# Linear attention beside softmax attention: two projections beside each of the first attention blocks, then stages of the linear attention beside the other blocks

## The chip, the cores and the metric

The kernel runs on one core of one Trainium2 chip. The metric is the device time of one execution in microseconds (us). A core has a matrix engine (PE in the profile; its loads of stationary operands are the engine PEld), a vector engine (DVE), a scalar engine for functions and copies (ACT), a general engine (POOL), and a queue that issues DMAs (SP). Each engine works through its own list of instructions in order, and waits where an operand isn't there yet. SBUF is the working memory of 128 partitions, PSUM the memory that PE writes into.

## The reference

One step of a two-layer network over 128 context tokens and 1024 latent tokens (1152 columns in all), width 1024, float32. The change lies in layer 0, whose mixer is this:

```python
def even_lat(h, kc, vc, s0, w_in, sink, w_alpha, b_alpha, gla_gain, w_out):
    qa, ka, va, qb, kb, vb, rb, lr = even_project(h, w_in)          # one projection, split
    oa = latent_attention(rope_2d(qa), rope_2d(ka), va, kc, vc, sink)   # 8 heads, blocks of 128
    ob, _, _ = gla_bidir(qb, kb, vb, lr, w_alpha, b_alpha, s0[:, 0], s0[:, 1])   # 4 heads
    return jnp.concatenate([oa, gla_output(ob, rb, gla_gain)], axis=-1) @ w_out

def gla_chunked(q, k, v, log_a, s0):          # chunks of 64 tokens, once forward, once backward
    bcum = jnp.cumsum(ac, axis=3)
    q_e, k_e, k_s = qc * exp(bcum), kc * exp(-bcum), kc * exp(b_last - bcum)
    attn = where(mask, einsum('nbhid,nbhjd->nbhij', q_e, k_e), 0)
    o_intra = einsum('nbhij,nbhjv->nbhiv', attn, vc)
    kv = einsum('nbhjd,nbhjv->nbhdv', k_s, vc)
    # scan over the chunks: o_inter = q_e @ s;  s = decay_last * s + kv
    return o_intra + o_inter, s_fin

def gla_output(o, r, gain):                   # o: tokens x 4 heads x 128
    o = o * rsqrt(mean(o * o, axis=-1) + EPS)
    return o.reshape(B, T, B_WIDTH) * gain * silu(r)
```

Every layer also has shifts, scales and gates from a map of the conditioning vector (48 units of the matrix `w_ada`), and a feed-forward part after the mixer.

## The kernel before

Activations lie with the features on partitions and the 1152 tokens along the free side, as 128 x 1152 tiles in slots `u0` to `u33`. A projection (`proj`) is three chunks of 384 tokens, each 24 matmuls (lines 148 to 150: float32 is split into a high and a low part, three products per 128 features), into one of three PSUM buffers `mm`.

The stretch that the change touches comes after the first projections:

- A loop of nine calls, `attention(i - 1)` for the context block and the eight latent blocks. A call takes two groups of four heads through score matmuls (L777 to L789, into `S`), mask and maximum (L794), exponentials (L803), division (L810), transposes (L815, into `X`), a split into high and low part (`split`, L144 and L145) and the products with the values (L826 to L828, into the one buffer `O`). Beside each of the first eight calls stands one projection with `ev_spill` (the q and k of the linear attention, then its gates r), which goes to HBM, and two units of the conditioning map (`ada_step(2)`). The projections read `H`, which holds slots u0 to u15.
- The linear attention (GLA) of four heads, each in stages. `gla_a` loads q, k, v and the decays, forms the scaled keys (ACT, POOL), transposes them and makes the chunk states KV (L902, L917, copies L929 on ACT and DVE). `gla_b` scans the states over the chunks: four DVE scans of 64 x 1152 (L943, L944), two for each half of the value width. `gla_c` makes the products within the chunks (L963), masks them (L966), and sums them with the products of the states (L972, L975) in `O`. `gla_d` squares the result, sums over the 128 features by a matmul with ones, takes the root, spreads it over partitions by a matmul (`rstd_r` L230, `rstd_b` L240), and multiplies by gain and by silu of the gate. Before the change only `gla_a(0)` stands in the loop, in its last round; the rest follows it, with units of the conditioning map (`ada_step(6)`) and the output product of the softmax heads (`out_a`, four calls of 72 matmuls with residual adds, `resid`, L318) in between.
- A unit of the conditioning map (`ada_unit`) loads two 512 KB pieces of `w_ada` into a ring of buffers, five before the change (three of the tiles `raw`, which `wload` also uses for weights, and c0, c1), and does eight small matmuls (L193) and two with the matrix `sel` (L199). Forty units run in this stretch: eighteen in the loop, the others after it.

The program is written in that order, but a scheduler of the framework sets the order of the instructions on each engine, by its own timing model and by which buffers are free, and puts in all waits. The order it made is fixed in the program.

## Time and profile before

| | us |
|---|---|
| median of 3 runs (2879.07 to 2884.31) | 2879.49 |
| the profiled execution | 2881.95 |
| its span in the trace | 2880.2 |
| PE busy / DVE busy / ACT busy / POOL busy in the span | 2712.5 / 2023.1 / 1329.0 / 1277.9 |
| mean granted clock of TensorE, of full speed | 0.957 |

The profile page lists for each engine how long it was busy; a PE record lasts longer than the distance to the next one, since matmuls overlap, so the work of PE is read from the starts of successive instructions. Tables by stretch give the busy time of each engine, the number of its instructions, and PEclk, the granted clock of TensorE as a share of its full speed (1.00 is 2.4 GHz, 0.50 is 1.2 GHz).

### The profile page before, as it was taken

Reading aid. Unit: us, or ns where it says so; the run is one execution under the profiler, and the core shown is the slowest. Engines: PE = TensorE matmul, PEld = TensorE weight load, DVE = VectorE, ACT = ScalarE, POOL = GpSimd, SP = SyncE. Lnnn points to the kernel's source line nnn. Section 1 sums busy time; section 2 is a strip of 40 time slices with the busy share of each in tenths; the row PEclk is TensorE's granted clock in tenths of the full one; section 3 lists DMA queues with packets and bytes.
Section 4 is the critical chain, followed back from the end, with each engine's and each line's share of the span. In section 5 each row is a group of like instructions: output and inputs, shape, how many; then the busy total and the mean of one; then the engine's idle time right before and its main releaser. Section 6 shows DMA issues by size and latency. Waiting matters only on the chain.

```text
span 2880.2 us, 48645 instructions
## 1 busy us (share of the span) xinstructions
PE 2712.5 (94%) x18792; PEld 2608.1 (91%) x18792; DVE 2023.1 (70%) x3509; ACT 1329.0 (46%) x2329; POOL 1277.9 (44%) x768
## 2 busy tenths in 40 slices
PE   7999997989899999999999989786899999999998
PEld 5888885878899999999999989786899999999998
DVE  5465667554588778778777565657788877787876
ACT  5445555533544444435335566574543433444333
POOL 4230005222655555456555433333455556455453
PEclk9999997788999999999999999998999999999999
DMA  7124347444153222623223123364342233423322
GB/s 272 64 91 162 122 134 258 146 148 147 67 204 104 81 88 89 227 81 94 90 88 125 54 89 114 122 224 145 112 170 85 87 98 108 171 88 105 104 82 70
DMA packets 138120, 353.67 MB, mean 123 GB/s; under 512 B 14720, under 2 KB 64256, under 8 KB 137888
## 3 DMA queue, kind: packets, MB, share of 16 engines
q1 hardware_dynamic: 136160, 343.48, 36.2%
q0 software_dynamic: 1728, 7.08, 0.7%
q8 instruction: 148, 2.42, 0.3%
q14 instruction: 84, 0.69, 0.1%
HBM read 286.20 MB, written 64.30 MB: 122 GB/s over the span
## 4 chain that ended last, share of the span: by engine, by line
PE 73%; DVE 11%; ACT 6%; DMA 5%; issue 3%; POOL 1%; SPq 0%; DVEq 0%; ACTq 0%; POOLq 0%
PE mm L148 10%; PE mm L150 10%; PE mm L149 10%; PE X L148 5%; PE X L150 5%; PE X L149 5%; PE S L148 4%; PE S L150 4%; PE S L149 4%; PE O L148 2%; PE O L150 2%; PE O L149 2%; PE mm L193 1%; DMA raw<-in_w_fi_dram 1%; PE O L975 1%
## 5 line engine op out<-in xcount | busy, mean ns | idle before, releaser
L150 PE MATMUL mm<-u,w 128*128 128x384 f32 (+1 forms) x1320 | 424.3, 323 | 1.9 <-DVE w L459 1.9
L148 PE MATMUL mm<-u,w 128*128 128x288 f32 (+1 forms) x1234 | 401.4, 326 | 22.0 <-DVE u L318 21.7
L149 PE MATMUL mm<-u,w 128*128 128x288 f32 (+1 forms) x1234 | 396.8, 322 | 2.7 <-POOL u L145 2.7
L140 POOL TENSOR_TENSOR w<-raw,w 128x1024 fp32r<-128x1024 f32 (+1 forms) x66 | 148.8, 2254 | 369.7 <-ACT w L139 319.3
L148 PEld LDWEIGHTS mm<-u,w 128*128 128x128 f32 x1234 | 238.8, 194 | 28.9 <-issue 26.0
L150 PEld LDWEIGHTS mm<-u,w 128*128 128x128 f32 x1320 | 253.7, 192 | 6.0 <-issue 3.5
L149 PEld LDWEIGHTS mm<-u,w 128*128 128x128 f32 x1234 | 238.5, 193 | 3.4 <-POOL u L145 2.9
L150 PE MATMUL mm<-u,u 128*128 128x288 f32 x693 | 204.5, 297 | 0.0
L148 PE MATMUL S<-u,w 128*128 128x288 f32 (+1 forms) x526 | 163.6, 311 | 40.7 <-ACT t L1173 35.0
L318 DVE SCALAR_TENSOR_TENSOR u<-mm,mods,u 128x288 f32<-128x288 f32 (+4 forms) x345 | 146.6, 453 | 76.9 <-PE mm L150 76.4
L150 PE MATMUL X<-u,w 128*128 128x288 f32 (+1 forms) x630 | 192.0, 306 | 0.0
L148 PE MATMUL mm<-u,u 128*128 128x288 f32 x627 | 187.6, 299 | 3.7 <-ACT u L445 3.5
L149 PE MATMUL mm<-u,u 128*128 128x288 f32 x627 | 186.3, 297 | 0.0
L148 PE MATMUL X<-u,w 128*128 128x288 f32 (+1 forms) x580 | 175.9, 305 | 3.0 <-DVE u L145 2.4
L149 PE MATMUL X<-u,w 128*128 128x288 f32 (+1 forms) x580 | 175.5, 304 | 0.0
L149 PE MATMUL S<-u,w 128*128 128x288 f32 (+1 forms) x526 | 162.2, 308 | 0.0
L148 PE MATMUL mm<-u,c 128*128 128x288 f32 (+2 forms) x497 | 152.6, 307 | 0.7 <-DVE ta L506 0.7
L149 PE MATMUL mm<-u,c 128*128 128x288 f32 (+2 forms) x497 | 151.6, 305 | 0.4 <-POOL u L145 0.4
L452 POOL TENSOR_TENSOR u<-raw 128x512 f32<-128x512 f32 x82 | 133.4, 1627 | 34.4 <-DMA raw<-in_w_fi_dram 19.3
L148 PEld LDWEIGHTS S<-u,w 128*128 128x128 f32 x526 | 100.8, 192 | 43.5 <-ACT t L1173 37.1
L448 DVE TENSOR_TENSOR u<-u,raw 128x512 f32<-128x512 f32 x82 | 138.2, 1685 | 0.8
L148 PE MATMUL X<-u,u 128*128 128x288 f32 (+1 forms) x444 | 131.5, 296 | 1.1 <-DVE u L145 0.6
(437 smaller groups left out, 9195.6 us busy)
## 6 DMA issues: line engine op xcount, KB each, us to landing
raw<-in_w_fi_dram SPq DMA_DIRECT2D x164, 512.0 KB, 3.5
raw<-in_w_fo_dram SPq DMA_DIRECT2D x96, 384.0 KB, 3.1
raw<-in_w_ada_dram SPq DMA_DIRECT2D x48, 512.0 KB, 5.2
c<-in_w_ada_dram SPq DMA_DIRECT2D x32, 512.0 KB, 5.9
d_w<-u SPq DMA_DIRECT2D x20, 512.0 KB, 3.9
u<-d_w SPq DMA_DIRECT2D x20, 512.0 KB, 4.5
u<-in_w_ada_dram SPq DMA_DIRECT2D x16, 512.0 KB, 10.2
raw<-in_w_fo_dram SPq DMA_DIRECT2D x16, 512.0 KB, 3.8
```

Of the source, the lines that this page charges most:

```text
L140: gp.tensor_tensor(out=lo[:, :n], in0=raw[:, :n], in1=f_(hi[:, :n]), op=ALU.subtract)
L148: pe.matmul(ps, wh, hh, start=first, stop=False)
L149: pe.matmul(ps, wh, hl, start=False, stop=False)
L150: pe.matmul(ps, wl, hh, start=False, stop=last)
L193: pe.matmul(ps[32 * g:32 * g + 32, :256], scp[:, 4 * p + g], raw[:, g * 256:(g + 1) * 256], start=p == 0, stop=p == 1)
L318: ve.scalar_tensor_tensor(x, ps[:, s0:s1], mod(l, j, cond, n), x, op0=ALU.mult, op1=ALU.add)
L448: ve.tensor_tensor(out=s2, in0=s1, in1=a11, op=ALU.subtract)
L452: gp.tensor_tensor(out=s3, in0=a11, in1=a21, op=ALU.subtract)
L975: pe.matmul(po[:, oc:oc + 64], S(c), qt[:, c * 64:(c + 1) * 64], start=False, stop=c % 2 == 1)
```

## The change

- The loop runs two projections beside each of the first four attention calls, none beside the others. From the fourth on, stages of GLA stand in it: `gla_a(0)`; `gla_a(1)`; `gla_b(0)`; `gla_c(0)` and `gla_b(1)`; `gla_d(0)`, `gla_a(2)` and `gla_c(1)`; `gla_d(1)`. Heads 2 and 3 follow after the loop, in another order among `out_a` and `ada_step`.
- `gla_c` has its result with the tokens on partitions: the masked products and the q tile become the stationary operands (L971, L973 of the new file), v and the states stream. ACT then squares each block of 128 x 128 into the same PSUM buffer with a sum along the row (`gss`).
- `gla_d` loads the gate whole into u13, scales each block by its own row factor (ACT), transposes it back (L997) and multiplies by gain and gate in one DVE instruction per group. The matmuls of `rstd_r` and `rstd_b` go.
- `gla_a` uses the buffers `mm` in place of `S`; the two mask buffers become halves of u12; the attention's transposed tile uses c0 and u22 in place of u22 and u32.
- `ada_unit` has a ring of four (c0 is taken), and two transposes and a DVE sum in place of the two matmuls with `sel`.

```diff
-                    aring[0] = (aring[0] + 1) % 5
-                    raw = uc(aring[0] - 3) if aring[0] > 2 else pw.tile([128, D], F32, name="raw", bufs=3)
+                    aring[0] = (aring[0] + 1) % 4
+                    raw = uc(1) if aring[0] == 3 else pw.tile([128, D], F32, name="raw", bufs=3)
...
-                pe.matmul(ps2[:, 2 * c:2 * c + 2], th[:, c * 128:(c + 1) * 128], sel[:, 0:2], start=True, stop=True)
+                pe.transpose(ps[:, 256 + c * 128:384 + c * 128], th[:, c * 128:(c + 1) * 128], ident)
...
+            ve.tensor_reduce(m, ps[:, 256:512].rearrange("p (k g c) -> p c k g", k=2, g=4)[:, 0:2],
+                             axis=mybir.AxisListType.X, op=ALU.add)
+            ve.tensor_tensor(out=m, in0=m, in1=cols[:, None, b:b + 2].to_broadcast([128, 2, 2]), op=ALU.add)
...
-                    t = us(((11, 14) if b == 7 else (22, 32))[ptr[0] % 2], F32R)
+                    t = uc(0, F32R) if ptr[0] % 2 else us(22, F32R)
...
-                    pe.matmul(po[:, o:o + 128], vb3[:, b], at[:, o:o + 128], start=True, stop=False)
+                    pe.matmul(po[:, o], at[:, o], vb3[:, b], start=True, stop=False)
                     for c in (2 * b, 2 * b + 1):
-                        pe.matmul(po[:, oc:oc + 64], S(c), qt[:, c * 64:(c + 1) * 64], start=False, stop=c % 2 == 1)
+                        pe.matmul(po[c % 2 * 64:c % 2 * 64 + 64, o], qt[:, c * 64:(c + 1) * 64], S(c), start=False, stop=True)
                 sc.copy(o32[:, b0 * 128:b1 * 128], po[:, :nb * 128])
+                for b in range(b0, b1):
+                    sc.activation(out=po[:, o], in_=o32[:, b * 128:(b + 1) * 128], func=AF.Square, accum_out=ss[:, b:b + 1])
...
+                    sc.mul(o, o, ss[:, b:b + 1])
+                    pe.transpose(ps[:, (b - b0) * 128:(b - b0 + 1) * 128], o, ident)
+                ve.scalar_tensor_tensor(rt[:, g], ps[:, :(b1 - b0) * 128], gain, rt[:, g], op0=ALU.mult, op1=ALU.mult)
...
             attention(i - 1)
-            if i < 8:
-                proj(wload(A["w_ef"][6 + i]), H, ev_spill(d_qk[i], 0.125 if i < 2 else 1.0) if i < 4 else ev_spill(d_r[i - 4], None))
+            for n in range(2 * i, min(2 * i + 2, 8)):
+                proj(wload(A["w_ef"][6 + n]), H, ev_spill(d_qk[n], 0.125 if n < 2 else 1.0) if n < 4 else ev_spill(d_r[n - 4], None))
             ada_step(2)
-            if i == 8:
+            if i == 3:
                 gla_init()
                 gla_a(0)
+            if i == 4:
+                gla_a(1)
+            if i == 5:
+                gla_b(0)
+            if i == 6:
+                gla_c(0)
+                gla_b(1)
+            if i == 7:
+                gla_d(0)
+                gla_a(2)
+                gla_c(1)
+            if i == 8:
+                gla_d(1)
...
-        gla_b(0)
-        gla_a(1)
-        gla_c(0)
-        ada_step(6)
-        gla_b(1)
-        gla_d(0)
-        out_a(0)
-        gla_a(2)
-        gla_c(1)
         ada_step(6)
         gla_b(2)
-        gla_d(1)
-        out_a(2)
         gla_a(3)
+        out_a(0)
+        ada_step(6)
         gla_c(2)
-        ada_step(6)
         gla_b(3)
         gla_d(2)
+        out_a(2)
+        ada_step(100)
+        gla_c(3)
         out_a(4)
-        gla_c(3)
-        ada_step(100)
         gla_d(3)
         out_a(6)
```

What the scheduler makes of it is shown at two places. The first is DVE at the scans of head 0 (`SCALAR_TENSOR_TENSOR` of 64x1152; u0 is the state tile, u2 the decays, X and S are PSUM buffers, `ISA` on L793 or L794 is the attention's mask and maximum). Before, they stand behind the last attention block, among the linear attention's own instructions:

```order
L929 COPY u0_4422<-S_4441 64x4x128
L929 COPY u0_4422<-S_4454 64x128
L966 COPY_PREDICATED u12_4363<-mq_82,X_4644 128x512
L966 COPY_PREDICATED u12_4363<-mq_82,X_4645 128x512
L966 COPY_PREDICATED u13_4364<-mq_82,X_4671 128x512
L929 COPY u0_4422<-S_4455 64x128
L893 MEMSET dls0_85 64x1 x2
L943 SCALAR_TENSOR_TENSOR u0_4422<-u2_4538,u0_4422 64x1152 x2
L966 COPY_PREDICATED u13_4364<-mq_82,X_4672 128x512
L944 SCALAR_TENSOR_TENSOR u0_4422<-u2_4538,u0_4422 64x1152 x2
```

Now they stand in the middle of an attention block:

```order
L793 ISA u19_3728,small_79<-S_3744,u23_1784 128x512
L793 ISA small_79 128x1
L793 ISA u19_3728,small_79<-S_3750,u23_1784 128x512
L793 ISA small_79 128x1
L942 SCALAR_TENSOR_TENSOR u0_3354<-u2_3945,u0_3354 64x1152 x2
L892 MEMSET dls0_84 64x1 x2
L943 SCALAR_TENSOR_TENSOR u0_3354<-u2_3945,u0_3354 64x1152 x2
L145 TENSOR_TENSOR u22_3538<-X_3533,u22_3538 128x512
L799 SCALAR_TENSOR_TENSOR small_79<-small_79 128x2
L145 TENSOR_TENSOR c0_3549<-X_3544,c0_3549 128x512
```

The scans have moved between the maximum of one attention group and the splits of another. The second place is PE behind the loop, at the units of the conditioning map (raw, c0 and c1 are the ring; O, X and S PSUM buffers). Before, units stand among products of the linear attention, as here ahead of `out_a(2)`:

```order
L193 MATMUL mm_5197<-raw_5204,scp_74 32x256 x3
L963 MATMUL X_5507<-u3_4979,u4_4980 128x128
L963 MATMUL X_5506<-u3_4979,u4_4980 128x128
L963 MATMUL X_5507<-u3_4979,u4_4980 128x128
L963 MATMUL X_5506<-u3_4979,u4_4980 128x128
L917 MATMUL S_5065<-u15_4982,u2_5013 128x128
L193 MATMUL mm_5215<-raw_5216,scp_74 32x256 x4
L193 MATMUL mm_5215<-c0_5222,scp_74 32x256 x4
L193 MATMUL mm_5233<-c1_5234,scp_74 32x256 x3
L199 MATMUL mm_5197<-sel_75,t_5210 128x2 x2
```

Now the last ten units stand in one piece between `out_a(2)` and `out_a(4)`; its first rows:

```order
L192 MATMUL mm_5622<-raw_5623,scp_74 32x256 x4
L192 MATMUL mm_5622<-raw_5629,scp_74 32x256 x4
L192 MATMUL mm_5641<-c1_5642,scp_74 32x256 x4
L192 MATMUL mm_5641<-raw_5648,scp_74 32x256 x4
L197 MATMUL mm_5622<-ident_76,t_5635 128x128 x2
L197 MATMUL mm_5641<-ident_76,t_5654 128x128 x2
L192 MATMUL mm_5660<-raw_5661,scp_74 32x256 x4
L192 MATMUL mm_5660<-raw_5667,scp_74 32x256 x4
```

Nothing of the linear attention or of `out_a` stands between them any more. At the last matmul of the eight projections 278 of the 706 rows of attention matmuls are through, where it was 598 before.

## Rows read from the trace of the kernel before

**Rows 1.** Table by stretch: us, then busy (x instructions) per engine, clock, DMA share, GB/s.

```profile
183.00:427.00 244.00, 238.73 (x1585) 214.42 (x1584) 156.70 (x388) 119.70 (x288) 31.59 (x15) 0.99 0.40 133
427.00:472.00 45.00, 36.61 (x260) 24.76 (x260) 32.88 (x78) 27.15 (x66) 19.09 (x15) 0.95 0.98 314
472.00:716.00 244.00, 220.04 (x1341) 189.51 (x1340) 124.83 (x189) 99.46 (x165) 71.12 (x52) 0.76 0.46 151
...
900.00:1000.00 100.00, 100.00 (x758) 100.00 (x757) 82.75 (x149) 44.88 (x77) 60.49 (x32) 1.00 0.30 90
```

**Rows 2.** Timeline of PE in an attention block: start, us, instruction.

```profile
410.26 0.40 PE L827 MATMUL O<-u,u 128*128 128x512 f32 x1
410.50 0.40 PE L828 MATMUL O<-u,u 128*128 128x512 f32 x1
...
411.19 0.40 PE L787 MATMUL S<-u,u 128*128 128x256 f32 x2
411.43 0.40 PE L779 MATMUL S<-u,u 128*128 128x256 f32 x2
...
412.14 0.60 PE L815 MATMUL X<-ident,u 128*128 128x128 f32 x4
412.49 0.48 PE L787 MATMUL S<-u,u 128*128 128x256 f32 x2
```

**Rows 3.** Timeline of PE behind the loop.

```profile
687.75 1.05 PE L193 MATMUL mm<-raw,scp 128*32 128x256 f32 x16
688.73 0.49 PE L972 MATMUL O<-u,u 128*128 128x128 f32 x2
689.05 1.01 PE L975 MATMUL O<-u,u 128*128 128x64 f32 x4
689.90 0.44 PE L972 MATMUL O<-u,u 128*128 128x128 f32 x2
```

**Rows 4.** Groups by line, DVE, 232 to 440: xcount | busy, mean ns | idle before.

```profile
L145 DVE TENSOR_TENSOR u<-X,u 128x512 fp32r<-128x512 f32 x54 | 36.8, 687 | 22.3 <-ACT u L144 22.1
L794 DVE CUSTOM_DVE_ANT_0 u<-S,u 128x512 f32<-128x512 f32 x48 | 31.9, 687 | 15.4 <-PE S L787 13.9 <-PE X L815 1.2
L810 DVE TENSOR_SCALAR u<-u,small 128x512 f32<-128x512 f32 x48 | 22.4, 528 | 0.4
```

**Rows 5.** The same view of DVE, 420 to 735.

```profile
L944 DVE TENSOR_TENSOR_SCAN u<-u,u 64x1152 f32<-64x1152 f32 x8 | 24.2, 3030 | 0.1
L943 DVE TENSOR_TENSOR_SCAN u<-u,u 64x1152 f32<-64x1152 f32 x8 | 22.6, 2836 | 2.1 <-ACT u L940 1.7 <-POOL u L931 0.3
L882 DVE TENSOR_TENSOR u<-u 64x384 f32<-64x384 f32 x24 | 14.0, 582 | 6.1 <-DMA u<-d_b 4.7 <-PE S L902 0.9
L929 DVE COPY u<-S 64x512 f32<-64x512 f32 x12 | 13.5, 1121 | 14.9 <-ACT u L929 14.6
L966 DVE COPY_PREDICATED u<-mq,X 128x512 f32<-128x512 uint8 x16 | 11.6, 728 | 11.2 <-PE X L963 11.0
```

**Rows 6.** Timeline of DVE at the scans of head 2.

```profile
583.43 2.55 DVE L944 TENSOR_TENSOR_SCAN u<-u,u 64x1152 f32<-64x1152 f32 x1
586.00 4.82 DVE L943 TENSOR_TENSOR_SCAN u<-u,u 64x1152 f32<-64x1152 f32 x1
```

**Rows 7.** Timeline of POOL at the same scans.

```profile
585.16 3.25 POOL L895 TENSOR_TENSOR u<-u,u 128x1152 f32<-128x1152 f32 x1 [8.55 <-DMA u<-d_qk]
589.75 3.48 POOL L897 TENSOR_TENSOR u<-u,u 128x1152 f32<-128x1152 f32 x1 [1.34 <-ACT u L896]
```

**Rows 8.** Waits of PE, 472 to 716: us in total, times, longest.

```profile
PE S L240 <- DVE r L233: 7.7, 1, 7.7
```

**Rows 9.** Table by stretch behind the loop, columns as in rows 1.

```profile
580.00:597.00 17.00, 6.70 (x57) 4.90 (x50) 16.07 (x11) 10.67 (x14) 10.51 (x3) 0.70 0.77 256
597.00:621.00 24.00, 24.00 (x113) 22.64 (x113) 7.89 (x17) 0.94 (x3) 4.14 (x5) 0.71 0.13 42
...
701.00:716.00 15.00, 15.00 (x97) 15.00 (x96) 6.12 (x14) 9.18 (x15) 5.39 (x3) 1.00 0.68 226
```

More of the change, by code (lines that the diff above doesn't have):

```diff
@@ L64, in body @@
         scp = st.tile([128, 8, 32], F32, name="scp")
-        sel = st.tile([128, 32], F32, name="sel")
         ones = st.tile([128, 128], F32, name="ones")
@@ L75, in body @@
         dls0 = st.tile([128, 36], F32, name="dls0")
+        gss = st.tile([128, 18], F32, name="gss")
         pair = {}
@@ L911, in gla_a @@
             kv4 = KV.rearrange("p (v c two) -> p two c v", c=9, two=2)
-            for b0, b1 in GRP:
-                pp = [aux(), aux()]
+            for gi, (b0, b1) in enumerate(GRP):
+                pp = [aux("mm", 3) for hf in range(2)]
                 for b in range(b0, b1):
@@ L980, in gla_d @@
             gain = cols[:, C_GAIN + hd:C_GAIN + hd + 1]
+            rt = us(13)
+            sy.dma_start(out=rt, in_=d_r[hd])
+            sc.activation(out=rt, in_=rt, func=AF.Silu)
+            ss = gss[:, (hd % 2) * 9:(hd % 2) * 9 + 9]
+            sc.activation(out=ss, in_=ss, func=AF.Sqrt, scale=1.0 / 128, bias=epst[:, 0:1])
+            ve.reciprocal(ss, ss)
             if hd == 3:
                 OB[3] = (us(22, F32R), us(23, F32R))
[L983 to L994 removed]
+            for b0, b1 in GRP:
+                ps = aux("mm", 3)
+                g = slice(b0 * 128, b1 * 128)
+                for b in range(b0, b1):
+                    o = o32[:, b * 128:(b + 1) * 128]
+                    sc.mul(o, o, ss[:, b:b + 1])
+                    pe.transpose(ps[:, (b - b0) * 128:(b - b0 + 1) * 128], o, ident)
+                ve.scalar_tensor_tensor(rt[:, g], ps[:, :(b1 - b0) * 128], gain, rt[:, g], op0=ALU.mult, op1=ALU.mult)
                 if hd == 3:
[L996 removed]
+                    split(OB[3][0][:, g], OB[3][1][:, g], rt[:, g])
                 else:
[L998 removed]
+                    sy.dma_start(out=d_ob[hd][:, g], in_=rt[:, g])
         d_ob = dr.tile([3, 128, T], F32, name="d_ob")
```

31 lines of the change are left out of this document (7 added, 24 removed).

## The prediction

> **What bounds the kernel now.** I read the table by stretch first. Until 183 us nothing changes but the conditioning units, and behind 716 us, where the last matmul of `out_a` ends, the same work follows as before. Between them lie three stretches [rows 1]. In the first (244 us, attention with a projection beside each call) PE is the bound: busy for 238.7 us at clock 0.99, DVE for 157 of 244. In the second (45 us, the end of the attention, no projection left) no engine is full: DVE is busy 73% of it, and the DMA engines are (share 0.98, 314 GB/s). In the third (244 us, linear attention and `out_a`) DVE is at 51%, ACT at 41%, and the clock at 0.76. The third is where time lies. The closer table shows its pattern [rows 9]: 17 us in which PE works for 6.7 and DVE for 16.1 (the scans), then a call of `out_a` that takes 24 us at clock 0.71, where the last call takes 15 us at 1.00. The waits say the same: PE stands 7.7 us for a tiny reciprocal that is queued behind scans [rows 8]. The scans of one head are in a chain with its copies before and its masks behind, and in this stretch nothing else feeds PE meanwhile.
>
> The three stretches are 533 us. The sum is made for them, as A (until the eight projections are through), B (rest of the attention) and C (until `out_a` is through).
>
> **A: projections with fewer attention blocks.** The matmuls of the projections stay. By the order of instructions attention goes from 598 to 278 of 706 rows in A, so 45% of it moves out. Attention has 31 pairs of query block and key block (1, 3, six times 4, 3), 7.75 full blocks of four; 45% are 3.5 blocks. A full block is 32 score matmuls at 0.12 us (two in 0.24), 32 transposes at 0.0875 (four in 0.35) and 24 products at 0.24 [rows 2]: 3.8 + 2.8 + 5.8 = 12.4 us of PE. That is 43 us. Eight conditioning units go too: 16 records of L193 take 0.98 us [rows 3], with the copy's matmuls some 1.3 us a unit, 11 us. Since PE is the bound in A, A = 244 - 43 - 11 = **190 us**. Where two projections stand beside a block, DVE has half the work per matmul, so I see nothing that takes PE's place.
>
> **B: attention with linear attention.** What is left is 4.75 full blocks without a projection. DVE per block: 8 splits and 8 maxima at 0.687, 8 divisions at 0.528 [rows 4] are 15.2 us, and 4 us for the small ones (the query split and the column operations, an estimate): 19.2, so 91 us. To this come, for three heads, `gla_a` (six L882 at 0.58, three L929 at 1.12, some 2.1 of smaller copies: 9 us each, 27 us), for two heads the scans (two of 2.84 and two of 3.03 each: 11.7, so 23.5 us), `gla_c` (L966: 3.5 each, 7 us) [rows 5], and `gla_d` with the new sums for fourteen conditioning units (9 us, an estimate). Together 158 us of DVE. PE has 4.75 x 12.4 = 59 us of attention, 18 of conditioning units and some 41 of linear attention: 118 us, less than DVE. ACT over all three stretches is busy 246 of 533 us [rows 1]; it gains squares and scalings of 128 x 128 blocks and loses the roots, so it isn't first either. B is bound by DVE, between 158 us (DVE never idle) and 216 us (the 73% of the stretch of today that is most like it). The highest share of DVE in a steady stretch of this trace is 0.83, in the feed-forward part [rows 1]; I take that, since two independent chains feed DVE here: 158 / 0.83 = **190 us**. In this place a scan that waits or runs delays what is queued behind it: the split of L145 and the small columns of the other attention group, and behind these ACT's exponentials and PE's products.
>
> Two things can push B up. POOL's multiplications of `gla_a` now run beside attention. A scan takes 2.55 us alone and 4.82 us where POOL multiplies in parallel [rows 6, 7]; the mean that I used (2.9) has a part of it. For three heads POOL has about 33 us of such work, and at the worst half of it, 16 us, is lost to DVE. The other is the load at the start of B: q, k, v and decays of two heads are 4.7 MB, 15 us at 314 GB/s, before the first stage can run, while attention goes on.
>
> **C: the tail.** PE at full clock: four calls of `out_a` at 12.7 us (the 15 us of [rows 9] less the small products in them) 51 us; twenty conditioning units at 1.2, 24 us; two heads of `gla_c`; `gla_a` and `gla_d` of what is left, 7 us. For `gla_c` a block of 128 tokens takes 0.32 + 0.85 us for L972 and L975 [rows 3] and some 0.4 for the masked products. Its four records of L975 take 0.21 each where L972 takes 0.16, although they stream half the columns; their stationary operand is the state tile, read with a step of 18 floats. In the change that tile is streamed and q is the stationary operand; the trace doesn't show that form. If the step costs as much when streamed, the block stays at 1.57 us and two heads take 28 us; if it costs nothing, at 0.16 a record, 1.36 and 24. I take 25. The sum is 107 us.
>
> [...]
>
> PE also waits in C. The last ten units stand in one piece; the ring holds two of them, and eight have to come through HBM at 1.05 MB each: 3.3 us a unit at 314 GB/s, 27 us, in which PE has 12: 15 us. And the scans of head 3 stand on DVE ahead of the residual adds of `out_a(0)`: three `mm` buffers are filled and PE waits for about one head's scans, 11 us. C = 107 + 15 + 11 = **133 us**, without the slow calls of `out_a`, since the scans that let the clock fall are over for heads 0 to 2.
>
> **The rest.** At the start eight units have transposes in place of the products with `sel` and one more small DVE sum; DMA sets the pace there. I take 0, 2 us at most either way. A ring of four instead of five matters in C alone.
>
> **Sum.** 190 + 190 + 133 = 513 us in place of 533, so 20 us less: the profiled execution of 2882 us would come to 2862. The median of the runs lies 2.5 us lower; I give **2860 us**.
>
> **Rivals.**
>
> *A larger gain.* B runs at 165 us (DVE at 96%), since the stages of GLA fill every hole, and the ring of C keeps up, 120 us. 190 + 165 + 120 = 475: 58 us less, 2822 us. For it: two chains that don't depend on each other; against it: no stretch of this trace has DVE above 0.83.
>
> *Slower: the queue of DVE.* In B the order is fixed, and attention's short steps stand behind scans of 2.5 to 5 us, so that PE and ACT wait, come back late and leave DVE idle in turn. If DVE stays at the 73% of the second stretch, and loses the 16 us to POOL, B is 174 / 0.73 = 238 us, and the sum 561: 28 us more, 2908 us. It decides from B = 210 us on, a DVE share of 75% for 158 us. For it: the second stretch is just this mix and has only 73%; against it: there DMA was full at 0.98 and two groups of attention were all that was left.
>
> *Slower: the clock.* PE has 118 us of work in B, some 62% of it. If the clock were at 1.2 GHz all through, PE would need 236 us and be the bound: 46 us more than my B, 26 us more in all, 2906 us. The second stretch speaks against it: PE at some 60% and still 0.95. [...]
>
> *No change.* B at 200 and C at 143 take the gain up. That the change doesn't do what it says is next to excluded by the order, which shows the scans inside the attention.
>
> **How the numbers follow.** Forecast (8 to 45 us less) 0.45, larger gain 0.21, no change 0.13, slower by DVE's queue 0.15, slower by the clock 0.05, something else slower 0.01. A difference of 0.2%, 6 us, is about what a measurement of this kernel can tell from none. So faster 0.66, within 0.2% 0.13, slower 0.21. The range goes from 2812 (a little past the larger gain) to 2898 (B at 225 us): some 0.1 lies below, 0.1 above.
>
> **What would show it.** In the profile after: the last matmul of the eight projections at about 373 us (A); the last attention product at about 563 us, with DVE at 0.8 or more and a clock near 1.00 between them (B); the last matmul of `out_a` at about 696 us, with waits of PE for `w_ada` in its last third (C). A clock of 0.6 to 0.7 in B would show the clock rival; DVE below 0.75 with waits of PE and ACT for L145 and the scans the queue. I am wrong in a step if A is over 200 us (then attention, not the projections, holds A), or if C is over 145 or under 120.

## The result, and the profile after

The change made the kernel slower: 2901.98 us (median of 4 runs, 2896.01 to 2904.8) against 2879.65 for the kernel before beside it, a ratio of 1.0071 (95% interval 1.0051 to 1.0092). The forecast was 2860 us, faster, with a range up to 2898. The profiled execution took 2896.01 us, its span is 2894.2. It is the fastest of the four, so the spans of the two kernels differ by 14 us where the medians differ by 22.

The table by stretch of the kernel after (us, then busy time and instructions of PE, PEld, DVE, ACT, POOL, then granted clock, DMA share, GB/s) answers to [rows 1]; the fourth row lies inside the third:

```profile
183.00:366.00 183.00, 177.41 (x1097) 164.79 (x1096) 96.88 (x213) 68.98 (x161) 33.21 (x15) 0.99 0.36 118
366.00:572.00 206.00, 164.97 (x1028) 117.20 (x1027) 160.39 (x351) 131.07 (x309) 45.56 (x38) 0.83 0.49 152
572.00:735.00 163.00, 133.56 (x878) 92.96 (x877) 51.00 (x114) 51.03 (x121) 30.83 (x25) 0.85 0.56 192
672.00:705.00 33.00, 22.85 (x184) 7.42 (x183) 4.32 (x23) 3.73 (x10) 0.00 (x0) 0.67 0.82 286
```

The last projection matmul starts at 366.2 us (marked at 373), the last attention product at 571.9 (563), the last matmul of `out_a` at 735.4 (696). Cut at these three starts, with the forecast beside them:

| | A | B | C | sum |
|---|---|---|---|---|
| before | 244.5 | 43.4 | 245.1 | 533.0 |
| forecast | 190 | 190 | 133 | 513 |
| after | 183.2 | 205.7 | 163.5 | 552.4 |

So A came out 7 us better, B 16 us worse and C 30 us worse. Of the 19 us by which the three are longer than before, 5 come back behind `out_a` (span less its end: 2158.8 us, before 2164.2). In B no engine is full: PE at 80%, DVE at 78%, clock 0.83. In C it is PE at 82% and clock 0.85. The fourth row is the piece of ten conditioning units: 33 us in which PE has 23 of work, most of that at clock 0.50, and the DMA engines a share of 0.82. The timeline of PE there (start, us, instruction, in brackets the wait ahead of it and what ended it):

```profile
677.45 0.64 PE L192 MATMUL mm<-raw,scp 128*32 128x256 f32 x8 [1.90 <-DMA raw<-in_w_ada_dram]
680.56 1.08 PE L192 MATMUL mm<-raw,scp 128*32 128x256 f32 x8 [2.47 <-DMA raw<-in_w_ada_dram]
682.14 0.69 PE L197 MATMUL mm<-ident,t 128*128 128x128 f32 x2 [0.49 <-ACT t L195]
682.75 1.08 PE L192 MATMUL mm<-c,scp 128*32 128x256 f32 x8
683.61 1.08 PE L192 MATMUL mm<-raw,scp 128*32 128x256 f32 x8
685.24 0.69 PE L197 MATMUL mm<-ident,t 128*128 128x128 f32 x2 [0.55 <-ACT t L195]
```

Eight records take 0.64 us at 677 and 1.08 from 680 on: behind waits of 1.9 and 2.5 us for `w_ada` the clock is at its lower level (0.97 in the stretch 677 to 680, 0.50 in 680 to 690), and a unit then takes 3.1 us (682.14 to 685.24), of which 0.55 us are a wait for ACT's copy.

**PE's time by clock.** For each stretch I added up the distances between the starts of successive PE instructions (no more of each than its duration), apart for the two levels of the granted clock; the rest is time in which PE issued nothing. The clock records of the two kernels have no other levels than 1.00 and 0.50. In the kernel before, matmuls of 128x288 and 128x384 that follow one another start 0.133 and 0.173 us apart at 1.00, and 0.240 and 0.320 at 0.50. So 96 columns more take 0.040 us at one level and 0.080 at the other, 2.4 and 1.2 columns per ns: these are the 2.4 and 1.2 GHz of the forecast and the expectations. A matmul of 128x384 as a whole takes 1.85 times as long at 0.50; halving the time at 0.50, as I do below, is an estimate and takes off somewhat more than this ratio would.

| us | at clock 1.00 | at clock 0.50 | nothing issued | the same work at 1.00, by halving |
|---|---|---|---|---|
| B after (206) | 105 | 60 | 41 | 135 |
| C after (163) | 93 | 41 | 29 | 113 |

In C the forecast had 107 us of PE work and 26 us of waits (15 for `w_ada`, 11 for the scans of head 3): the trace has 113 and 29. What the sum lacked altogether is the lower clock; by halving, 41 us at clock 0.50 are 21 us more than at 1.00. This is a count and at most a price, since a stretch gets shorter only where PE is what it waits for. The waits also have other shares than in the forecast (PE in C: us, times, longest):

```profile
PE mm L192 <- DMA raw<-in_w_ada_dram: 8.2, 6, 2.5
PE mm L197 <- ACT t L195: 6.9, 9, 2.1
PE O L973 <- DVE u L943: 2.8, 1, 2.8
```

Cut at the piece of ten units, with the terms of the forecast sorted by place, and PE's time in the kernel after:

| us of C | forecast | after | at clock 1.00 | at clock 0.50 | nothing issued |
|---|---|---|---|---|---|
| ahead of the piece (572 to 672) | 80 | 100 | 62 | 20 | 18 |
| the piece (672 to 705) | 27 | 33 | 6 | 17 | 10 |
| behind it (705 to 735) | 25 | 30 | 25 | 4 | 2 |

In B the forecast had 158 us of DVE, and the trace has 160; there the share is off, 0.78 and not 0.83. PE's work in B is 135 us by this count, where the forecast had 118.

### The profile page after: what moved, and what is told of

It is laid out like the page before. It is cut to its first block, busy times and chain, and to the rows that moved or that the text cites. A ratio compares the mean times of both kernels' runs of the same rounds, so it can differ in the third digit from the quotient of the medians.

```text
span 2894.2 us, 48346 instructions
## 1 busy us (share of the span) xinstructions
PE 2686.5 (93%) x18588; PEld 2546.2 (88%) x18588; DVE 2016.1 (70%) x3536; ACT 1333.6 (46%) x2403; POOL 1270.5 (44%) x767
## 4 chain that ended last, share of the span: by engine, by line
PE 67%; DVE 13%; ACT 7%; DMA 7%; issue 4%; POOL 2%; SPq 0%; DVEq 0%; ACTq 0%; POOLq 0%
PE mm L150 9%; PE mm L148 9%; PE mm L149 9%; PE X L148 5%; PE X L150 5%; PE X L149 5%; PE S L148 4%; PE S L150 4%; PE S L149 4%; PE O L148 2%; PE O L150 2%; PE O L149 2%; DMA raw<-in_w_fi_dram 1%; PE mm L192 1%; DVE u L317 1%
## 5 line engine op out<-in xcount | busy, mean ns | idle before, releaser
L150 PE MATMUL mm<-u,w 128*128 128x384 f32 (+1 forms) x1320 | 422.3, 322 | 3.5 <-DVE w L458 1.9
L149 PE MATMUL mm<-u,w 128*128 128x288 f32 (+1 forms) x1234 | 395.0, 321 | 3.2 <-POOL u L145 3.2
L140 POOL TENSOR_TENSOR w<-raw,w 128x1024 fp32r<-128x1024 f32 (+1 forms) x66 | 147.6, 2239 | 384.5 <-ACT w L139 334.5
L150 PEld LDWEIGHTS mm<-u,w 128*128 128x128 f32 x1320 | 252.7, 192 | 7.9 <-issue 2.9
L149 PEld LDWEIGHTS mm<-u,w 128*128 128x128 f32 x1234 | 237.4, 193 | 3.8 <-POOL u L145 3.4
L150 PE MATMUL mm<-u,u 128*128 128x288 f32 x693 | 204.1, 296 | 1.6 <-POOL u L445 1.6
L150 PE MATMUL X<-u,w 128*128 128x288 f32 (+1 forms) x630 | 192.0, 306 | 0.0
L149 PE MATMUL mm<-u,u 128*128 128x288 f32 x627 | 185.3, 296 | 0.0
L149 PE MATMUL X<-u,w 128*128 128x288 f32 (+1 forms) x580 | 175.6, 304 | 0.0
L149 PE MATMUL S<-u,w 128*128 128x288 f32 (+1 forms) x526 | 161.6, 307 | 0.0
L149 PE MATMUL mm<-u,c 128*128 128x288 f32 (+2 forms) x497 | 151.6, 305 | 0.0
L447 DVE TENSOR_TENSOR u<-u,raw 128x512 f32<-128x512 f32 x82 | 144.4, 1761 | 0.8
L150 PEld LDWEIGHTS mm<-u,u 128*128 128x128 f32 x693 | 130.8, 189 | 2.5 <-POOL u L445 2.5
```

Source lines behind the costliest of these rows:

```text
L140: gp.tensor_tensor(out=lo[:, :n], in0=raw[:, :n], in1=f_(hi[:, :n]), op=ALU.subtract)
L149: pe.matmul(ps, wh, hl, start=False, stop=False)
L150: pe.matmul(ps, wl, hh, start=False, stop=last)
L447: ve.tensor_tensor(out=s2, in0=s1, in1=a11, op=ALU.subtract)
```

## The experiments

The theory after this comparison: in C the loads of the units set the pace because ten units stand in one piece. Its rivals: the new forms cost by themselves (rival 1); the stages of the linear attention in B hold up attention on DVE's queue (rival 2). All ratios are to runs of the kernel before on the same chip, with 95% intervals. A, B and C are of each run's profiled execution, cut as above. That is one execution, up to 8 us off the run's median, so a few us between two rows are scatter.

| run | A | B | C | sum | median us | ratio |
|---|---|---|---|---|---|---|
| forms | 256.8 | 45.1 | 219.8 | 521.7 | 2868.79 | 0.9979 [0.9963, 0.9995] |
| forms5 | 237.9 | 48.4 | 214.5 | 500.8 | 2846.29 | 0.9898 [0.9875, 0.9920] |
| before4 | 253.4 | 45.5 | 256.2 | 555.1 | 2892.49 | 1.0053 [1.0031, 1.0074] |
| projs | 185.7 | 124.6 | 222.8 | 533.1 | 2876.74 | 1.0006 [0.9988, 1.0024] |
| projs5 | 180.2 | 127.5 | 216.9 | 524.6 | 2870.06 | 0.9974 [0.9957, 0.9991] |
| noload | 184.3 | 204.7 | 144.7 | 533.7 | 2877.88 | 1.0006 [0.9989, 1.0023] |
| spread | 183.7 | 203.8 | 132.9 | 520.4 | 2865.60 | 0.9972 [0.9956, 0.9988] |
| adab | 188.3 | 227.0 | 126.0 | 541.3 | 2877.09 | 1.0010 [0.9992, 1.0027] |
| noscan | 183.9 | 190.2 | 165.0 | 539.1 | 2883.15 | 1.0019 [1.0002, 1.0036] |
| obuf | 187.5 | 198.5 | 179.5 | 565.5 | 2910.25 | 1.0116 [1.0086, 1.0146] |
| divpool | 182.8 | 218.0 | 164.5 | 565.3 | 2909.73 | 1.0102 [1.0085, 1.0118] |
| fill | 188.6 | 214.2 | 173.5 | 576.3 | 2916.53 | 1.0139 [1.0115, 1.0163] |
| forms5p | 235.1 | 48.5 | 225.1 | 508.7 | 2860.45 | 0.9929 [0.9914, 0.9944] |
| mix | 235.9 | 51.1 | 221.4 | 508.4 | 2875.23 | 0.9992 [0.9977, 1.0007] |

### The parts of the change one by one: forms, forms5, before4, projs, projs5

**forms**: the kernel after with the loop and the tail in the old order.

```diff
-            for n in range(2 * i, min(2 * i + 2, 8)):
+            for n in range(i, min(i + 1, 8)):
...
-            if i == 3:
+            if i == 8:
                 gla_init()
                 gla_a(0)
...
```

> The new forms alone (tokens on partitions, squares on ACT, transposes in the conditioning units, ring of four, shared PSUM buffers), in the old order: one projection beside each call, linear attention and out_a after the loop as before. If the forms themselves cost the time (rival 1), this run is 10 to 25 us above the kernel before, 2890 to 2905 us. If the order costs it, by the units' loads behind the loop (theory) or by the queue of DVE beside the attention (rival 2), this run stands within 6 us of the kernel before or below it, 2868 to 2885 us, with A at 244 us.

It is 0.2% faster than before: rival 1 falls, the forms don't cost the time. C falls from 245 to 220 us. But A, which was to stay at 244, rises to 257.

**forms5**: the same with the attention's transposed tile back in u22 and u32, and so c0 back in the ring.

```diff
-                    aring[0] = (aring[0] + 1) % 4
-                    raw = uc(1) if aring[0] == 3 else pw.tile([128, D], F32, name="raw", bufs=3)
+                    aring[0] = (aring[0] + 1) % 5
+                    raw = uc(aring[0] - 3) if aring[0] > 2 else pw.tile([128, D], F32, name="raw", bufs=3)
```

> The new forms in the old order, with the old five ring buffers for w_ada (the attention's transposed tile back in u22 and u32). With the ring of four, A took 257 us where the kernel before takes 244. If the ring is what A loses by, A comes back to 244 to 248 us and the kernel to 2856 to 2862 us; if the transposes and the sum of a unit, or the shared PSUM buffers, are, A stays at 254 us or more and the kernel at 2864 to 2874 us.

It beats both kernels, 1.0% faster than before; A is 238 us, below the kernel before and below the 244 to 248 us expected if the ring was all that A lost by.

```profile
183.00:421.00 238.00, 234.78 (x1553) 211.52 (x1551) 156.43 (x390) 119.21 (x283) 32.38 (x15) 0.99 0.41 138
469.00:684.00 215.00, 177.61 (x1210) 127.26 (x1211) 123.51 (x190) 99.85 (x234) 77.58 (x51) 0.85 0.53 178
```

PE works for 234.8 of A's 238 us. In its tail PE is busy for 178 us where [rows 1] have 220: the matmuls of the norm are gone, and the clock is 0.85 where it was 0.76.

**before4**: the kernel before with a ring of four (`% 4`, c1 alone beside `raw`), nothing else.

> The kernel before with a ring of four buffers for w_ada in place of five, nothing else. If the ring is what the new forms lost in A (257 us against 238 with five), A is 256 to 264 us here, where the kernel before has 244, and the kernel at 2891 to 2900 us. If that difference was one of the order that the scheduler made, and not of the ring, A is 240 to 250 us and the kernel within 6 us of 2879.

A is 253 us, between the two expectations: in this execution, 6 us above its median, the ring by itself costs 9 us there with one projection beside each call, and C 11 more; by the medians it costs 12 us in all. It thus explains about half of the 19 us between forms and forms5. The other half isn't shown: these two differ in the buffers of the attention's transposed tile as well, and so in the order that the scheduler made. In the kernel after A doesn't suffer (183 us): by the trace six units stand in it, not fourteen. The change with a ring of five was not run.

**projs**: the new forms and two projections beside each of the first four calls, the linear attention after the loop in the old order. **projs5**: the same with the ring of five.

> Of the change in order only the first half: two projections beside each of the first four calls, nothing beside the other five, and the linear attention after the loop in the old order. A is 183 us as in the kernel after. The attention left has 4.75 blocks; with DVE at the 78% of the kernel after it takes 91 / 0.78 = 117 us, and the old tail 244 us follows: 544 us, 11 us above the kernel before, 2891 us. If putting the linear attention beside the attention is what loses (rival 2), this run is the faster of the two, by 10 us or more against the kernel after; if the units behind the loop are (theory), it lies within 12 us of the kernel after on either side, since both pay for something else: here for attention alone.

> The new forms with the old ring of five and two projections beside each of the first four calls; the linear attention after the loop in the old order. It differs from the run of the new forms with five buffers (2846 us; A 238, B 48, C 214) by the projections' place alone. Theory: what attention loses without a projection beside it (124.6 us for 4.75 blocks in the run with a ring of four) isn't won back in A: A 184, B 125, C 214, sum 523 where that run has 501, so 22 us more, 2862 to 2870 us. If the two projections beside a call cost nothing by themselves, within 6 us of 2846.

projs took 2876.74 us where 2891 was expected, 25 us less than the kernel after. By its own expectation this is the sign of rival 2, not of the theory. But the expectation had the tail at 244 us, and with the new forms it takes 223; and the kernel after differs from projs in two things at once, the stages in the loop and the units in one piece. spread, below, parts them. projs5 came out as the theory had it (2870.06 us, sum 525 where 523 was expected). Against forms5 it differs in the place of the projections alone, and this costs 24 us of the three stretches (0.8% by the ratios): attention alone takes 127.5 us for its 4.75 blocks. The table of projs for its B:

```profile
368.70:493.00 124.30, 109.02 (x714) 76.96 (x713) 97.32 (x278) 85.67 (x205) 20.30 (x13) 0.93 0.62 194
```

DVE is at 97.32 / 124.3 = 0.78, the share that it has in the kernel after with the linear attention beside. B of the kernel after is 81 us longer (205.7 to 124.6) for 63 us more of DVE.

### The units behind the loop: noload, spread, adab

**noload**: the last ten units work on one resident tile. Left out are their loads, and so the values of these units.

```diff
+                elif still:
+                    raw = still[0]
...
-                sy.dma_start(out=raw, in_=A["w_ada"][l, u, p])
+                if not still:
+                    sy.dma_start(out=raw, in_=A["w_ada"][l, u, p])
...
+        still.append(uc(0))
+        ve.memset(still[0], 0.0)
         ada_step(100)
```

> The kernel after with the last ten conditioning units computed from one resident tile, without their twenty loads of 512 KB (left out: the loads, so the values of these units). Theory (the loads of the units set the pace behind the loop): the ten units go from 3.2 us each to 1.3, 19 us, and the weights of out_a(4) and out_a(6) no longer queue behind them, up to 7 us more: C from 165 to 139 to 146 us, the kernel at 2876 to 2883 us. Rivals 1 and 2 (forms, queue of DVE): the products of heads 2 and 3 take over as the last to come, and the gain stays under 6 us, 2896 us or more.

C falls by 18.8 us, to 144.7, and the kernel to 2877.88: the theory's numbers. Here are the stretches ahead of the piece and of the piece itself, first of the kernel after, then of noload (columns as above; the piece of the kernel after is the fourth row of the first table):

```profile
572.00:672.00 100.00, 82.58 (x545) 58.60 (x544) 37.47 (x71) 41.27 (x104) 21.12 (x20) 0.90 0.52 182
572.00:675.00 103.00, 86.66 (x545) 61.82 (x544) 38.28 (x72) 41.95 (x105) 23.45 (x21) 0.78 0.50 178
675.00:690.00 15.00, 13.38 (x184) 7.03 (x183) 3.83 (x21) 5.38 (x12) 2.36 (x1) 1.00 0.21 64
```

The gain lies in the piece, 15 us at clock 1.00 where it was 33 at 0.67, and behind it. So the waits for `w_ada` bring the lower clock with them here: 0.67 over the piece with its loads, 1.00 without. Ahead of the piece PE does the same 545 instructions in both kernels, in a slightly different order: the clock is 0.90 in one and 0.78 in the other, and the length 100 and 103 us. There the lower clock is hardly a price.

**spread** does all the work, with the units after each group of twelve matmuls of `out_a`:

```diff
                     resid(0, 2, X, n, c * CW, CW, ps)
+                    ada_step(1)
...
-        ada_step(6)
         gla_b(2)
...
-        ada_step(6)
         gla_c(2)
...
-        ada_step(100)
         gla_c(3)
```

> The kernel after with the twenty-two units behind the loop moved: one after each group of twelve matmuls of out_a, none in a piece. All work is done. Theory (the units' loads set the pace because they stand in one piece): twelve matmuls and a unit take 2.1 + 1.3 us of PE, the load of a unit 3.3, so C falls to that of the run without loads, 145 us plus or minus 5, and the kernel to 2878 plus or minus 6 us. If a shared buffer or the traffic as such is the cause and not the place, the loads of out_a's groups wait all the same and C stays above 157 us, the kernel above 2890.

C falls further than without the loads and than expected, to 132.9 us. Its table and the timeline of PE, of which I leave out the rows of L149 and L150:

```profile
570.00:703.00 133.00, 122.40 (x910) 85.37 (x910) 52.73 (x113) 48.01 (x118) 36.81 (x23) 0.95 0.66 227
```

```profile
652.52 0.38 PE L197 MATMUL mm<-ident,t 128*128 128x128 f32 x2
652.83 1.07 PE L192 MATMUL mm<-raw,scp 128*32 128x256 f32 x16
653.83 0.44 PE L148 MATMUL mm<-u,w 128*128 128x384 f32 x1
...
656.14 0.64 PE L192 MATMUL mm<-c,scp 128*32 128x256 f32 x8
656.59 0.61 PE L192 MATMUL mm<-raw,scp 128*32 128x256 f32 x8
657.14 0.44 PE L197 MATMUL mm<-ident,t 128*128 128x128 f32 x2
```

The DMA engines move 227 GB/s where the kernel after had 192, PE waits for `raw` with `w_ada` 0.9 us in all (8.2 in the kernel after), and the clock is 0.95. By the count of PE's time: 113 us at clock 1.00, 9 at 0.50, 11 without issue. Beside the kernel after that is 18 us less idle time and, by halving, 16 us less slow clock, with 4 us more work. So the place of the units, not their traffic, was the cost; how much of it was the clock such a count can't tell, as noload shows ahead of the piece. Behind `out_a` spread takes 9 us more than the kernel after (2167.4 us to 2158.8), which takes back part of the gain.

spread also answers the question that projs left open. With the stages beside the attention and the units spread the kernel is 0.3% faster than projs (0.9972 to 1.0006, intervals that just touch; 2865.60 us to 2876.74), although spreading the units loses in the old order (forms5p, below). So the stages in the loop by themselves aren't what loses time. But spread is no faster than forms either (0.9972 and 0.9979, intervals that overlap): with the same forms and ring, the new order at its best here is worth no more than the old one.

**adab** moves fifteen of them into B instead (`ada_step(2 if i < 4 else 5)`, none of the pieces of six).

> The kernel after with five conditioning units instead of two beside each of the last five calls, so that fifteen units move from behind the loop into B, where the DMA engines had a share of 0.49. Theory (loads): C falls by 15 times some 2.5 us, to about 128 us, and B rises by the units' small work on DVE, 15 times 0.5, to about 214: 2902 - 37 + 8 = 2873 us. Rival 2 (the queues in B are the loss): every unit put into B costs there what it saves in C, B goes to 225 us or more, and the sum stays at 2895 to 2905 us.

C fell as expected (126 us), but B rose by 21 us and not by 8, in an execution 8 us above its median. By the trace B holds 27 units where it held 14.5, so a unit costs 1.7 us there, though PE has 41 us without issue. These fell to 29, and PE's time at clock 0.50 rose from 60 to 80 us. The kernel is 2877 us, between the theory's 2873 and rival 2's 2895.

### What holds B: noscan, obuf, divpool, fill

**noscan** leaves out the eight scans of heads 0 and 1:

```diff
-                ve.tensor_tensor_scan(kv[F], D0[F], kv[F], 0.0, op0=ALU.mult, op1=ALU.add)
+                if hd > 1:
+                    ve.tensor_tensor_scan(kv[F], D0[F], kv[F], 0.0, op0=ALU.mult, op1=ALU.add)
```

> The kernel after without the eight scans of heads 0 and 1 (left out: the chunk states are not scanned, so the output of these heads is another one), some 23 us of DVE in B. If DVE's queue sets B (rival 2: DVE is 78% busy, and what stands behind a scan is late), B falls by 23 / 0.78 = 30 us, to 176, and the kernel to 2872. If B is the sum of chains in which DVE is one link of several, B falls by what DVE is busy with the scans or less, 15 to 23 us, to 183 to 191. If the scans are hidden, as the prediction had meant them to be, by no more than 10 us.

B falls by 15.5 us, less than DVE was busy with them, as expected for chains in which DVE is one link of several. This is how DVE spent B in the kernel after (busy us, mean ns, idle ahead):

```profile
L942 DVE TENSOR_TENSOR_SCAN u<-u,u 64x1152 f32<-64x1152 f32 x6 | 15.2, 2568 | 0.2 <-ACT u L939 0.2
L943 DVE TENSOR_TENSOR_SCAN u<-u,u 64x1152 f32<-64x1152 f32 x6 | 15.0, 2543 | 0.0
L145 DVE TENSOR_TENSOR u<-X,u 128x512 fp32r<-128x512 f32 x19 | 13.1, 688 | 6.5 <-ACT u L144 6.4
L965 DVE COPY_PREDICATED u<-mq,X 128x512 f32<-128x512 uint8 (+1 forms) x13 | 7.7, 601 | 8.1 <-PE X L962 7.0 <-PE mm L916 1.0
```

Three heads are scanned in B, not two, at 2.55 us a scan: the eight left out are 20.5 us, of which three quarters came off B. No scan shows the 4.82 us of [rows 6]: the loss to POOL that the forecast feared didn't come. But the trace doesn't put it to the test. During the scans of the three heads POOL (the numbers just before the clock) was idle but for 0.66 us:

```profile
405.20:415.40 10.20, 5.66 (x60) 4.15 (x50) 10.12 (x9) 3.90 (x12) 0.00 (x0) 0.91 0.63 221
439.60:449.90 10.30, 5.58 (x49) 2.84 (x48) 10.20 (x10) 3.02 (x9) 0.00 (x0) 0.83 0.90 312
543.00:553.30 10.30, 6.71 (x52) 3.38 (x41) 10.26 (x5) 6.77 (x25) 0.66 (x2) 1.00 0.92 300
```

DVE isn't evenly loaded: 56.7 of 60 us in 380 to 440, where the scans of two heads lie, 22.8 of 40 in 480 to 520. The share of 0.78 is a mean over such parts.

```profile
380.00:440.00 60.00, 46.82 (x266) 35.23 (x267) 56.70 (x112) 44.48 (x92) 12.22 (x8) 0.76 0.39 119
480.00:520.00 40.00, 34.16 (x217) 24.65 (x218) 22.77 (x56) 23.88 (x68) 11.87 (x10) 0.96 0.36 99
```

**obuf** gives the sums of `gla_c` the buffers `mm` (`po = aux("mm", 3)`) in place of `O`.

> The kernel after with the sums of gla_c in the three buffers mm and not in O, of which there is one and which attention uses too. If B is long because attention and gla_c wait for one another's O (the squares hold it longer now), B falls from 206 us by 8 us or more, to 198 or less, and the kernel to 2894 or less. If B is long because each stage adds its own chain, whatever it writes to, B stays within 4 us of 206 and the kernel within 5 us of the kernel after, 2897 to 2907.

B is 7 us shorter and C 16 longer: the kernel loses. The order of PE's instructions changed, in B and behind the loop, so the run says only that a buffer of its own doesn't win time; what of B's 7 us is the buffer I can't tell.

**divpool** does every second division in B on POOL.

```diff
-                    ve.tensor_scalar(P[i], P[i], den[:, i:i + 1], None, op0=ALU.mult)
+                    (gp if b > 2 and i % 2 else ve).tensor_scalar(P[i], P[i], den[:, i:i + 1], None, op0=ALU.mult)
```

> The kernel after with every second division of the attention's weights (128x512, 0.53 us on DVE) on POOL in the calls of B: 19 of them leave DVE, 10 us. If DVE's queue sets B (rival 2), B falls from 206 by 10 / 0.78 = 13 us, to 193, and the kernel to 2889. If B is a sum of chains, in which the division stands between the exponentials and the transposes wherever it runs, B falls by no more than 5 us, since POOL takes about twice as long for one, and the kernel stays at 2896 or more.

B rose by 12 us, which neither side had expected. A division on POOL takes 1.76 us in the mean of 16 of 128x512 and four of 128x384, more than three times the 0.53 of [rows 4]. The "about twice" of the expectation was an estimate; in the kernel before, an operation of 128x512 takes 1.27 us on POOL (L968) and 0.69 on DVE (L145). The divisions of the run:

```profile
L809 POOL TENSOR_SCALAR u<-u,small 128x512 f32<-128x512 f32 (+1 forms) x20 | 35.0, 1757 | 66.4 <-DVE small L807 53.5 <-ACT t L195 12.4 <-ACT O L978 0.5
L809 POOL TENSOR_SCALAR u<-u,small x20: 1234/1562/3610, 383.3 to 550.8; 128x512 f32<-128x512 f32 x16, 128x384 f32<-128x384 f32 x4
```

The longest of them (second row: least, median and most ns) ran beside scans. Of the sixteen divisions of 128x512 left on DVE eight took 0.75 to 1.19 us, each of them beside one on POOL, the others 0.48. So DVE lost 7 us of work and not 10, and PE's order in B changed too. That a chain that got longer cost more than a queue that got shorter gave back fits this, and so does the disturbance; the run doesn't part them. It shows only that this way of relieving DVE loses.

**fill** gives PE 128 matmuls of 128x512 that nothing reads.

```diff
+                if b > 2:
+                    fill()
                 po = aux("O", 1)
                 for kb in range(nk):
...
+                if hd < 2:
+                    fill()
                 po = aux("O", 1)
```

> The kernel after with 128 more matmuls of 128x512 in B that nothing reads, eight ahead of the products of each of ten attention groups and of the first six groups of gla_c: 31 us of PE at 0.24 each. In the kernel after PE spends 60 of B's 206 us on instructions that run at 1.2 GHz, which would be 30 at 2.4. If those 30 us are a cost that a busier PE wins back, the granted clock of B goes from 0.83 to 0.93 or more and B stays at 206 plus or minus 10 us in spite of the 31. If B is long only by its chains and the clock follows, what is put in adds its own time, as the conditioning units did (1.4 us each): B goes to 228 us or more and the kernel to 2922 or more.

```profile
372.00:586.00 214.00, 189.30 (x1145) 137.83 (x1144) 161.72 (x351) 129.32 (x307) 45.62 (x37) 0.90 0.45 140
```

The result lies between the two. Some 32 us of added PE work lengthen B by 8.5; the clock rises from 0.83 to 0.90, and PE's time at clock 0.50 falls from 60 to 43 us, by halving 8.5 us. The rest went into time in which PE had issued nothing (41 us, now 25). So B has slack on PE that independent matmuls can use. That B would be shorter at a higher clock isn't shown, since it got longer. C is 10 us longer in this run, and the kernel is 0.7% above the kernel after by the ratios.

### Can the tail be filled better: forms5p, mix

**forms5p** is forms5 with one unit after each group of `out_a`, as in spread. **mix** is forms5 with each `out_a` straight behind the scans:

```diff
         gla_b(0)
+        out_a(0)
         gla_a(1)
         gla_c(0)
```

> The best order so far (new forms, ring of five, one projection beside each call, linear attention after the loop) with the twenty-two units behind the loop placed one after each group of twelve matmuls of out_a. In this order the units stand already in pieces of six among the linear attention's products, where PE has pauses. If it is the spreading that helps wherever it is done, C falls from 214 us to 200 or less and the kernel to 2832 or less. If a unit in a pause of PE is worth as much as one beside out_a, within 6 us of 2846; if PE's pauses stay open, since nothing fills them, C rises to 225 or more and the kernel to 2857 or more.

> The best order so far (new forms, ring of five, 2846 us; C 214) with each call of out_a straight behind the scans of one head (gla_b), so that its 72 matmuls stand beside the scans and gla_a of the next head. In C of that kernel PE spends 54 us on instructions at 1.2 GHz, 27 more than at 2.4. If work that needs no DVE chain fills PE's pauses and holds the clock, C falls by 10 to 30 us, to 185 to 204, and the kernel to 2816 to 2836 us. If the residual adds queue behind the scans on DVE (three mm buffers are filled in 6 us) and PE stops there, C stays within 8 us of 214 or rises.

Both lose against forms5, forms5p 0.3% and mix 0.9% by the ratios. In forms5p C rises to 225 us: the units had stood in pauses of PE, and these are open now. In mix `out_a` ends later (C 221 us), and units and `gla_d(3)` still stand behind it, where 19 us more are spent than in forms5. The waits of PE in its C (us, times, longest):

```profile
PE mm L916 <- DVE u L928: 15.2, 6, 7.1
PE O L973 <- DVE u L943: 13.4, 3, 4.9
```

The copies and scans of the linear attention come late on DVE, as the expectation had put it for the other outcome. forms5 stays the best version.

## Why the prediction was wrong, point by point

**A (190, measured 183): right.** PE was the bound at clock 0.99. What moved out was 61 us, some more than the 54 priced. That a ring of four "matters in C alone" was wrong: A is 185.7 us in projs and 180.2 in projs5, and the loss is larger where more units stand in A (before4, forms).

**B (190, measured 206): the DVE work was right (158, measured 160), the share was the wrong step.** The 0.83 came from the feed-forward stretch in [rows 1], where PE is full and DVE follows it. That row says nothing of what DVE can reach where chains of DVE, ACT and PE alternate. There it is 0.73 in [rows 1], 0.78 with attention alone (projs) and 0.78 with the linear attention beside. "Two independent chains feed DVE" was the reason given, and the trace shows that the second chain didn't raise the share. The argument that no stretch has DVE above 0.83 overlooked the scans (16.07 of 17 us in [rows 9]). That the work came out right is in part luck: three heads were scanned and not two, at 2.55 us and not 2.9, and other terms were smaller.

Of the rivals, DVE's queue at 0.73 plus the POOL loss (238) is not what came: the share is 0.78, and no loss to POOL shows. That DVE's work is part of what holds B noscan does show, 15.5 us for 20.5 us of scans. The clock rival was priced as all or nothing (236 us); what came is a part of it, 60 us of PE's time at clock 0.50. The second stretch, which the forecast held against this rival, has PE busy 36.61 of 45 us in [rows 1], 81% and not some 60%. How much of B's 16 us is the clock stays open: 30 us is the most by halving, and no run shortened B by raising the clock alone. Why DVE stays at 0.78 is open too. Of the range, B at 225 us gives 2895 us by the forecast's own sum, not 2898.

**C (133, measured 163.5): waits foreseen, clock left out.** The ten units in one piece and their 15 us of waits were in the sum, and noload measures 19 for their loads, the slow clock behind the waits included. The failed step is "without the slow calls of `out_a`, since the scans that let the clock fall are over for heads 0 to 2". It put PE's time at clock 0.50 at nothing, and it was 41 us, at most 21 us of the 30: 17 in the piece and 4 behind it, where the waits for `w_ada` bring it (noload has clock 1.00 in both), and 20 ahead of the piece. Ahead of it lies most of the miss, 100 us where the terms give 80, with 18 us without issue where 11 were foreseen; what sets these 100 us no run shows. In the piece the loads set much of the pace by themselves: eight units of 1.05 MB at the 286 GB/s measured there are 29 of its 33 us, an estimate.

The run spread, which has the work without the piece, has C = 133 us. That this is the forecast's number is chance: there it is 118 us of work, 11 without issue and 4 or 5 of slow clock, not 107 and 26.

**The streamed state tile (25 us for two heads of `gla_c`): between the bounds, for another reason.** The timeline of PE at clock 1.00; in the fourth row the same timeline cut off at 641.34 us, when two records of L973 have begun; then all records of the two lines (least, median and most ns):

```profile
640.91 0.49 PE L971 MATMUL O<-u,u 128*128 128x128 f32 x2
641.33 0.68 PE L973 MATMUL O<-u,u 128*64 128x128 f32 x4
641.93 0.49 PE L971 MATMUL O<-u,u 128*128 128x128 f32 x2
641.33 0.43 PE L973 MATMUL O<-u,u 128*64 128x128 f32 x2
L973 PE MATMUL O<-u,u x144: 421/424/477, 488.6 to 649.6; 128*64 128x128 f32 x144
L971 PE MATMUL O<-u,u x72: 275/362/582, 488.2 to 649.1; 128*128 128x128 f32 x72
```

A block takes 1.02 us where [rows 3] give 1.17; with the forecast's 0.4 for the masked products it is 1.42, between its 1.36 and 1.57, and two heads take 25.6 us. The four products with the stepped tile take 0.60 us, 0.15 each, but they start two by two, within 0.01 us of each other: the two chunks of a block write 64 partitions each, and the records of such a pair, 0.42 us long, lie side by side. The forecast didn't have this. One record by itself takes 0.42 us, longer than most of L971, which stream an unstepped tile of the same size. So the 0.15 doesn't say that the step is free. No run here parts the step from the pairing.

**What wasn't priced at all.** The forms alone take 31 us out of the old tail (C 245 to 214.5 in forms5), more than the whole gain forecast; the sum counted PE's work of the new C from the start and never asked what the forms give in the old order. Seen so, the change in order as it stands throws away what the forms bring: by sums of the three stretches, forms5 500.8, with the ring of four 521.7, with two projections beside a call 533.1, with the stages in the loop and the units in a piece 552.4.

**No change, larger gain:** neither came. C did reach 133 us in spread and 126 in adab, but B stood at 204 and 227.

## What to carry to other kernels

An engine's share of busy time is taken from a stretch with the same bound: DVE at 0.83 beside a full PE is no price for a stretch in which PE and DVE wait for each other. A wait of PE is idle time and can bring the slow clock for the work behind it (the piece, 33 us at clock 0.67 with its loads and 15 at 1.00 without; what of the difference is the clock isn't parted). The second is a price only where PE sets the pace: ahead of the piece a clock of 0.78 for 0.90 went with 3 us of 100. Loads that can't be hidden belong in small pieces between long runs of matmuls, not in one block, unless they stand in pauses that nothing else fills (forms5p). Before work is moved beside a chain, ask what covered that chain until now: here the projections covered attention, and nothing covered it after.

## What the runs showed that I had not expected

A ring of buffers one shorter costs the kernel before 0.5% (before4, 2892 us), though the buffer taken away serves the conditioning units alone. The matmuls of `gla_c` with 64 stationary columns, whose results go to different halves of the partitions, start in pairs: four took 0.60 us, though each record lasts 0.42. A scan of 64x1152 took 2.55 us on DVE in the mean of the kernel after, with POOL busy for 0 to 0.66 of the 10 us of a head's four scans. Beside operations of two tiles on POOL (L895, L897, then L140) it took 4.8 us, not once but twice:

```profile
590.83 4.81 DVE L944 TENSOR_TENSOR_SCAN u<-u,u 64x1152 f32<-64x1152 f32 x1
```

This is the kernel before, the next scan after those of [rows 6]. In the kernel after, POOL was idle during nearly all scans; no run was made to bring this about.
